# Eight recurrent scans moved into the attention's steps, and post-norms that multiply by their weights ahead of the scale

## The chip, the cores and the metric

The kernel runs on one core of one Trainium2 chip. A core has five engines with queues of their own: TensorE (PE in the profile; its weight loads are PEld), VectorE (DVE), ScalarE (ACT), GpSimd (POOL) and SyncE (SP, which here only issues transfers). Each engine works its queue in order and waits on semaphores for the others. The metric is the device time of one execution in microseconds; the kernel before takes 1060.09 us (median of 3 runs, 1060.06 to 1060.18).

## What is computed

Two encoder layers over a sequence of 512 tokens of 1024 channels in float32. Layer 0 mixes with attention and a recurrent branch side by side, layer 1 with a two-dimensional Fourier transform; each is followed by a SwiGLU. All four sublayers have a norm before and one after:

```python
x = x + rmsnorm(m, ln_mix_post[l])                 # m: the mixer of rmsnorm(x, ln_mix_pre[l])
x = x + rmsnorm(swiglu(hn, w_ffn_gate[l], w_ffn_up[l], w_ffn_down[l]), ln_ffn_post[l])

# attention of layer 0: 4 heads, two softmax maps each
p = jax.nn.softmax(s - slopes * dist, axis=-1)
a = p[:, :, 0] - lam * p[:, :, 1]
# recurrent branch: for a forward and a backward direction
a = jnp.exp(log_a)
u = jnp.sqrt(-jnp.expm1(2.0 * log_a)) * (i * x)
_, h = lax.associative_scan(_lin_combine, (a, u), axis=1, reverse=reverse)   # h[t] = a[t] h[t-1] + u[t]
rec = (h_fwd + h_bwd) * jax.nn.gelu(yg)
```

The recurrence has 512 channels, four tiles of 128, and two directions: eight scans over 512 positions. Attention and `rec` are joined and multiplied by the output matrix.

## The kernel before

Every matrix product is done in three matmuls (`mm3`, lines 108 to 111): each operand is split into a high part (`hi`, rounded) and a rest (`lo`), and hi*hi, hi*lo and lo*hi are added in PSUM. `split` (lines 100 to 106) makes the two parts: ACT casts (line 103, the `whi`, `qk`, `aT` of the profile), then DVE or POOL subtracts (line 106, `wlo`, `qk`, `aT`). Weights arrive as `raw` tiles by SP's queue and are split a few units ahead of their use; for units 8 to 13 (`LO_POOL`) the subtraction is POOL's, not DVE's.

Layer 0 goes in this order: pre-norm; projections for v, the recurrent input and its gates (`make_gates`); the decays (`lru_decay`, DVE, lines 487 to 489); the projection of q and k for heads 0 and 1 (`proj_qk(0)`); the square roots (ACT) and `ix*q` (POOL, line 497, `lru_root`). Then comes the attention loop, one step for each of 4 heads and 4 blocks of 128 queries, 16 steps (lines 680 to 690). A step i does:

- `scores`: six PE matmuls into two score banks (`psc`, line 550); DVE adds the bias and takes the row minimum (`p`, line 554, one for each map); ACT's exp (line 93); DVE's reciprocal and factor `c` (lines 558, 559), and one combination of the two maps (line 560)
- half of a filler product, 12 matmuls: heads 2 and 3's q and k in steps 0 to 7 (`pqk`), the GeLU gate's projection in steps 8 to 15 (`pyg`)
- in steps 0 to 3 two scans (`lru_scan`, line 502 forward, 505 backward); behind each backward one POOL adds the two directions (line 506, `hsum`)
- `finish_step`: the product with v for step i-3 if that is an odd block (`poT`, 12 matmuls), the transposition of step i-2's probabilities (`paT`, line 572, then an ACT cast and a DVE subtraction into `aT`), and now and then the head's norm and its transposition (`norm_o`, `turn_o`)

A scheduler lays this program out on the engines' queues by its own estimate of when things will be ready; it may place an instruction earlier or later than the code's order as long as the data allow. `order_after` (line 80) adds an edge that it must keep. PSUM has 8 banks, handed out in turn.

After the loop come the output projection, the first SwiGLU, the Fourier layer and the second SwiGLU, all bound to long chains of matmuls. Each ends in `proj_tok`, which finishes its four token tiles one after another and calls `post_norm` (line 255) for each: ACT squares both halves out of PSUM and sums, DVE scales the sum to the mean (lines 215, 216), POOL raises it to -0.5 (line 209), DVE multiplies each half out of PSUM by that and by the weights (line 265) and adds it to x (line 266). `pre_norm` or `pre_norm_tok` follows on the same tile, and in the last one the output transfers (line 860, all on SP).

Of the kernel before, what the change touches and what calls it, by code (L numbers as in the profile page):

```python
# [25 lines left out]
EPS = 1e-6  # L26
# [9 lines left out]
def encoder_kernel(  # L36
# [55 lines left out]
    def act(out_, in_, func, name, **kw):  # L92
        ins = A.activation(out_, in_, func, **kw)  # L93
# [27 lines left out]
    xt = [xpool.tile([P, D], F32, name=f"x{t}", tag=f"x{t}") for t in range(NT)]  # L121
# [79 lines left out]

    ident = const.tile([P, P], F32, name="ident")
    make_identity(nc, ident)
    mhalf = const.tile([P, 4], F32, name="mhalf")
    V.memset(mhalf, -0.5)

    def inv_sqrt(m):
        r = sm("r")
        G.tensor_tensor(out=r, in0=m, in1=mhalf[:, 0:1], op=ALU.pow)  # L209
        return r  # L210

    def inv_rms(ssa, ssb, n):

        m0, m = sm("m"), sm("m")
        V.tensor_scalar(out=m0, in0=ssa, scalar1=n * EPS, scalar2=None, op0=ALU.add)
        V.tensor_scalar(out=m, in0=ssb, scalar1=m0, scalar2=1.0 / n, op0=ALU.add, op1=ALU.mult)  # L216
        return inv_sqrt(m)

    def pre_stats(t, junk):
        ss = [sm("ss"), sm("ss")]  # L220
        for h in range(2):
# [33 lines left out]
    def post_norm(t, ps, g):  # L255

        ys = pair("y")
        ss = [sm("ss"), sm("ss")]
        for h in range(2):
            A.activation(ys[h], ps[h], AF.Square, accum_out=ss[h])  # L260
        r = inv_rms(ss[0], ss[1], D)
        for h in range(2):
            sl = slice(h * S, (h + 1) * S)
            y = ys[h]
            V.scalar_tensor_tensor(out=y, in0=ps[h], scalar=r, in1=g[:, sl], op0=ALU.mult, op1=ALU.mult)
            V.tensor_tensor(out=xt[t][:, sl], in0=xt[t][:, sl], in1=y, op=ALU.add)
# [103 lines left out]
    for name, ap in (  # L370
# [8 lines left out]
        n = ap.shape[0]  # L379
# [119 lines left out]
    def lru_scan(d, c):  # L499
        a_, q, u = lru_ac.pop((d, c))  # L500
        if d == 0:
            V.tensor_tensor_scan(out=u, data0=a_, data1=u, initial=0.0, op0=ALU.mult, op1=ALU.add)
            hsum[c] = u
        else:
            V.tensor_tensor_scan(out=u[:, ::-1], data0=a_[:, ::-1], data1=u[:, ::-1], initial=0.0, op0=ALU.mult, op1=ALU.add)  # L505
# [4 lines left out]
    bias = {}  # L510
# [25 lines left out]
    probs = {}  # L536
    sums = {}

    def scores(h, t):

        q_, k_ = qks[h]
        pr = pair("p")
        if t == 0:
            sums[h] = sm("sums", 8)
        s_ = sums[h]

        ps = [bank("psc"), bank("psc")]
        for n, (i, j) in enumerate(((0, 0), (0, 1), (1, 0))):
            for m, sl in enumerate(halves):
                T.matmul(ps[m], lhsT=q_[i][sl, t * P:(t + 1) * P], rhs=k_[j][sl, :], start=n == 0, stop=n == 2)  # L550
        for m in range(2):

            mn = sm("mn")
            V.tensor_tensor_reduce(out=pr[m], in0=ps[m], in1=bias[h][:, 384 - t * P:384 - t * P + S],  # L554
                                   op0=ALU.add, op1=ALU.min, scale=-1.0 / math.sqrt(QK), scalar=3.0e38, accum_out=mn)
            act(pr[m], pr[m], AF.Exp, "exp", scale=-1.0, bias=mn, accum_out=s_[:, m * NT + t:m * NT + t + 1])
        c1 = sm("c1")
        V.reciprocal(c1, s_[:, NT + t:NT + t + 1])
        V.scalar_tensor_tensor(out=c1, in0=c1, scalar=nlam, in1=s_[:, t:t + 1], op0=ALU.mult, op1=ALU.mult)
        V.scalar_tensor_tensor(out=pr[0], in0=pr[1], scalar=c1, in1=pr[0], op0=ALU.mult, op1=ALU.add)  # L560
        probs[h, t] = pr[0]
# [89 lines left out]
    lru = [(d, c) for c in range(4) for d in range(2)]  # L651
# [8 lines left out]
    n = len(steps)  # L660

    def finish_step(i):

        def step(lag):
            return steps[i - lag] if 0 <= i - lag < n else (None, None)

        h, t = step(3)
        if h is not None and t % 2:
            av(h, t // 2)
        h, t = step(2)  # L670
        if h is not None:
# [184 lines left out]
    proj_tok(range(8), lambda k: fT[k], 2, 6, fin1, turn_x)  # L856

    def after1(t):
        for h in range(2):
            nc.sync.dma_start(out[t * P:(t + 1) * P, h * S:(h + 1) * S], xt[t][:, h * S:(h + 1) * S])  # L860
# [63 lines left out]
```

## Time and profile before

| what | value |
|---|---|
| median of 3 runs | 1060.09 us (1060.06 to 1060.18) |
| the profiled execution's own time | 1061.07 us |
| its span, first to last instruction | 1059.2 us |
| mean granted TensorE clock | 0.992 |
| PE busy | 1027.0 us, 97% of the span |
| DVE busy | 478.0 us, 45% |
| ACT busy | 380.7 us, 36% |
| POOL busy | 100.1 us, 9% |

The span is what the trace shows; the execution's own time has 1.87 us more around it. A row of the timeline gives start, duration, engine, line, operation and tiles, and in brackets the idle time ahead of it with the instruction that ended it. Rows that merge several instructions end in xN. Matmuls overlap their neighbours, so the distance from one start to the next tells their pace. A row of the view by stretches gives, after its length, the busy time of each engine (number of instructions), then the granted clock (1.00 is full), the DMA share and GB/s. A row of the groups gives busy time and mean nanoseconds of one instruction, and the idle time ahead of them.

### The profile page before, as it was taken

What the parts mean: (1) busy time and instruction counts of PE and PEld (TensorE: products, weight loads), DVE (VectorE), ACT (ScalarE), POOL (GpSimd) and SP (SyncE); (2) the same over time, 40 slices, a digit from 0 to 9 for tenths busy, and PEclk for the clock granted to TensorE, in tenths of its full rate; (3) what the DMA queues carried; (4) which work ended last, traced back from release to release, by engine and by line L of the source; (5) the groups of instructions that cost most, each with busy time, mean ns of one, the idle gap of its engine ahead of it and who ended that gap; (6) DMA issues with size and microseconds to landing.
All of it is one profiled execution on the core that took longest, in us unless ns stands there. A gap on an engine that the chain in (4) does not pass through costs nothing.

```text
span 1059.2 us, 12273 instructions
## 1 busy us (share of the span) xinstructions
PE 1027.0 (97%) x4945; PEld 856.9 (81%) x4945; DVE 478.0 (45%) x720; ACT 380.7 (36%) x628; POOL 100.1 (9%) x94
## 2 busy tenths in 40 slices
PE   5999699999999999999999999999999999999997
PEld 5897577779888888888888888898888888888885
DVE  5969767754542322223333456645322223234304
ACT  5385456733532221123233445334321123223201
POOL 1058423211000000000100110100000000000000
PEclk9999899999999999999999999999999999999999
DMA  6531212321652343222533015027243223224002
GB/s 221 164 118 56 87 48 83 112 66 41 188 170 80 93 127 99 80 80 80 164 115 119 1 60 160 1 80 218 84 136 100 80 80 105 94 80 133 6 1 80
DMA packets 73123, 102.93 MB, mean 97 GB/s; under 512 B 3893, under 2 KB 61290, under 8 KB 73066
## 3 DMA queue, kind: packets, MB, share of 16 engines
q1 hardware_dynamic: 70442, 94.02, 28.4%
q0 software_dynamic: 2624, 8.13, 2.2%
q8 instruction: 39, 0.64, 0.2%
q14 instruction: 18, 0.15, 0.0%
HBM read 100.04 MB, written 2.10 MB: 96 GB/s over the span
## 4 chain that ended last, share of the span: by engine, by line
PE 86%; DVE 6%; ACT 4%; issue 1%; POOL 1%; DMA 1%; SPq 0%; POOLq 0%; DVEq 0%; ACTq 0%
PE pc L110 15%; PE pc L109 15%; PE pc L111 15%; PE pj L111 10%; PE pj L110 10%; PE pj L109 10%; ACT p L93 1%; ACT whi L103 1%; DVE gate L505 1%; DMA raw<-in_w_in_dram 1%; DVE p L560 1%; PE pT L250 1%; DVE wlo L106 1%; PE put L109 1%; PE put L110 1%
## 5 line engine op out<-in xcount | busy, mean ns | idle before, releaser
L106 DVE TENSOR_TENSOR wlo<-raw,whi 128x1024 fp32r<-128x1024 f32 x158 | 192.0, 1239 | 272.8 <-ACT whi L103 221.6
L110 PE MATMUL pc<-hnlo,whi 128*128 128x512 f32 (+1 forms) x768 | 285.2, 372 | 0.0
L109 PE MATMUL pc<-hnhi,whi 128*128 128x512 f32 (+1 forms) x768 | 284.6, 372 | 0.5 <-ACT hnhi L103 0.5
L111 PE MATMUL pc<-hnhi,wlo 128*128 128x512 f32 (+1 forms) x768 | 285.0, 371 | 0.0
L103 ACT CAST whi<-raw 128x1024 fp32r<-128x1024 f32 x164 | 167.9, 1050 | 121.4 <-PE pj L110 31.1
L110 PEld LDWEIGHTS pc<-hnlo,whi 128*128 128x128 f32 x768 | 144.7, 188 | 25.5 <-DVE hnlo L106 0.4
L109 PEld LDWEIGHTS pc<-hnhi,whi 128*128 128x128 f32 x768 | 144.2, 188 | 26.0 <-ACT hnhi L103 1.0
L111 PEld LDWEIGHTS pc<-hnhi,wlo 128*128 128x128 f32 x768 | 144.7, 188 | 24.6
L111 PE MATMUL pj<-whi,gs 128*128 128x512 f32 x352 | 137.0, 389 | 0.0
L109 PE MATMUL pj<-whi,gs 128*128 128x512 f32 x352 | 137.0, 389 | 0.0
L110 PE MATMUL pj<-wlo,gs 128*128 128x512 f32 x352 | 137.0, 389 | 0.0
L93 ACT ACTIVATE gated<-pc 128x512 f32<-128x512 f32 x44 | 26.2, 597 | 271.9 <-PE pc L111 271.9
L721 DVE TENSOR_TENSOR gated<-gated,pc 128x512 f32<-128x512 f32 x44 | 30.2, 686 | 113.3 <-PE pc L111 113.3
L109 PEld LDWEIGHTS pj<-whi,gs 128*128 128x128 f32 x352 | 66.1, 188 | 13.8
L111 PEld LDWEIGHTS pj<-whi,gs 128*128 128x128 f32 x352 | 66.1, 188 | 13.7
L110 PEld LDWEIGHTS pj<-wlo,gs 128*128 128x128 f32 x352 | 66.1, 188 | 13.6
L209 POOL TENSOR_TENSOR r<-m,mhalf 128x1 f32<-128x1 f32 x32 | 17.5, 545 | 552.3 <-DVE m L216 552.3
L260 ACT ACTIVATE y<-pj 128x512 f32<-128x512 f32 x32 | 19.1, 596 | 82.3 <-PE pj L111 82.3
L103 ACT CAST gs<-gated 128x512 fp32r<-128x512 f32 x44 | 25.3, 618 | 52.1 <-PE pj L110 32.2
L106 DVE TENSOR_TENSOR gs<-gated,gs 128x512 fp32r<-128x512 f32 x44 | 28.4, 685 | 31.3 <-ACT gs L103 31.3
L93 ACT ACTIVATE p<-p,mn 128x512 f32<-128x512 f32 x32 | 22.9, 719 | 37.5 <-DVE mn L554 37.5
L106 POOL TENSOR_TENSOR wlo<-raw,whi 128x1024 fp32r<-128x1024 f32 x12 | 28.8, 2407 | 51.5 <-ACT whi L103 51.5
(184 smaller groups left out, 1255.5 us busy)
## 6 DMA issues: line engine op xcount, KB each, us to landing
raw<-in_w_ffn_gate_dram SPq DMA_DIRECT2D x44, 512.0 KB, 3.9
raw<-in_w_ffn_up_dram SPq DMA_DIRECT2D x44, 512.0 KB, 4.9
raw<-in_w_ffn_down_dram SPq DMA_DIRECT2D x44, 512.0 KB, 3.4
raw<-in_w_in_dram SPq DMA_DIRECT2D x20, 512.0 KB, 3.8
raw<-in_w_mix_out_dram SPq DMA_DIRECT2D x8, 512.0 KB, 3.3
raw<-in_w_fourier_out_dram SPq DMA_DIRECT2D x8, 512.0 KB, 4.2
pos<-in_dft_pos_dram POOLq DMA_DIRECT2D x8, 256.0 KB, 5.1
out_dram<-x SPq DMA_DIRECT2D x8, 256.0 KB, 2.1
```

The source lines that it names most:

```text
L93: ins = A.activation(out_, in_, func, **kw)
L103: A.copy(hi, src)
L106: lo_eng.tensor_tensor(out=lo, in0=src, in1=f(hi), op=ALU.subtract)
L109: T.matmul(ps, lhsT=l[0], rhs=r[0], start=start, stop=False)
L110: T.matmul(ps, lhsT=l[0], rhs=r[1], start=False, stop=False)
L111: T.matmul(ps, lhsT=l[1], rhs=r[0], start=False, stop=stop)
L209: G.tensor_tensor(out=r, in0=m, in1=mhalf[:, 0:1], op=ALU.pow)
L250: T.transpose(pt[:, k * P:(k + 1) * P], xh[:, k * P:(k + 1) * P], ident)
L260: A.activation(ys[h], ps[h], AF.Square, accum_out=ss[h])
L505: V.tensor_tensor_scan(out=u[:, ::-1], data0=a_[:, ::-1], data1=u[:, ::-1], initial=0.0, op0=ALU.mult, op1=ALU.add)
L560: V.scalar_tensor_tensor(out=pr[0], in0=pr[1], scalar=c1, in1=pr[0], op0=ALU.mult, op1=ALU.add)
L721: V.tensor_tensor(out=gated[fc], in0=gated[fc], in1=ps, op=ALU.mult)
```

## The change

It has four edits.

1. The eight scans no longer stand two by two in steps 0 to 3 but one in each of steps 1, 2, 4, 5, 7, 8, 10 and 11, and each gets an order edge behind the last score tile (line 554) of its step, so that the scheduler can't pull it ahead.
2. The norms scale inside the square (ACT's `scale`, 1/sqrt(1024)), so that the mean is two plain additions.
3. `post_norm` multiplies PSUM by the weights first (a new DVE pass into `y`), squares into a scrap tile `junk`, and afterwards scales and adds in one pass on SBUF alone.
4. The second half of each output tile goes out by ACT's queue in place of SP's.

```diff
-    def inv_rms(ssa, ssb, n):
+    RD = 1.0 / math.sqrt(D)
+    def inv_rms(ssa, ssb):
-        m0, m = sm("m"), sm("m")
-        V.tensor_scalar(out=m0, in0=ssa, scalar1=n * EPS, scalar2=None, op0=ALU.add)
-        V.tensor_scalar(out=m, in0=ssb, scalar1=m0, scalar2=1.0 / n, op0=ALU.add, op1=ALU.mult)
-        return inv_sqrt(m)
+        m0, m, r = sm("m"), sm("m"), sm("r")
+        V.tensor_scalar(out=m0, in0=ssa, scalar1=EPS, scalar2=None, op0=ALU.add)
+        V.tensor_tensor(out=m, in0=ssb, in1=m0, op=ALU.add)
+        G.tensor_tensor(out=r, in0=m, in1=mhalf[:, 0:1], op=ALU.pow)
+        return r
...
     def post_norm(t, ps, g):
         for h in range(2):
-            A.activation(ys[h], ps[h], AF.Square, accum_out=ss[h])
-        r = inv_rms(ss[0], ss[1], D)
+            V.tensor_tensor(out=ys[h], in0=ps[h], in1=g[:, h * S:(h + 1) * S], op=ALU.mult)
+            A.activation(junk, ps[h], AF.Square, scale=RD, accum_out=ss[h])
+        r = inv_rms(ss[0], ss[1])
         for h in range(2):
-            V.scalar_tensor_tensor(out=y, in0=ps[h], scalar=r, in1=g[:, sl], op0=ALU.mult, op1=ALU.mult)
-            V.tensor_tensor(out=xt[t][:, sl], in0=xt[t][:, sl], in1=y, op=ALU.add)
+            V.scalar_tensor_tensor(out=xt[t][:, sl], in0=ys[h], scalar=r, in1=xt[t][:, sl], op0=ALU.mult, op1=ALU.add)
...
     def lru_scan(d, c):
+        order_after(sc, [last_score[0]])
...
-            V.tensor_tensor_reduce(out=pr[m], in0=ps[m], in1=bias[h][:, 384 - t * P:384 - t * P + S],
+            last_score[0] = V.tensor_tensor_reduce(out=pr[m], in0=ps[m], in1=bias[h][:, 384 - t * P:384 - t * P + S],
...
+    scans = list(lru)
     for i in range(n):
         scores(*steps[i])
-        if 2 * i < len(lru):
-            lru_scan(*lru[2 * i])
-            lru_scan(*lru[2 * i + 1])
+        if i % 3 and scans:
+            lru_scan(*scans.pop(0))
...
     def after1(t):
-        for h in range(2):
-            nc.sync.dma_start(out[t * P:(t + 1) * P, h * S:(h + 1) * S], xt[t][:, h * S:(h + 1) * S])
+        for h, q in enumerate((nc.sync, A)):
+            q.dma_start(out[t * P:(t + 1) * P, h * S:(h + 1) * S], xt[t][:, h * S:(h + 1) * S])
```

PE's queue is the same before and after. The first place is DVE's queue ahead of the first attention step. The scans are the rows that read and write one `gate` tile; `qk_140` is the rest of head 1's k, `p_141` is step 0's first score tile. Before:

```order
L106 TENSOR_TENSOR wlo_133_902<-raw_131_899,whi_132_901 128x1024
L502 SCALAR_TENSOR_TENSOR gate_85_551<-gate_85_551 128x512
L106 TENSOR_TENSOR wlo_136_908<-raw_134_905,whi_135_907 128x1024
L505 SCALAR_TENSOR_TENSOR gate_88_563<-gate_88_563 128x512
L106 TENSOR_TENSOR qk_138_936<-pqk_137_911,qk_138_936 128x512
L502 SCALAR_TENSOR_TENSOR gate_93_607<-gate_93_607 128x512
L505 SCALAR_TENSOR_TENSOR gate_96_619<-gate_96_619 128x512
L502 SCALAR_TENSOR_TENSOR gate_107_695<-gate_107_695 128x512
L505 SCALAR_TENSOR_TENSOR gate_110_707<-gate_110_707 128x512
L502 SCALAR_TENSOR_TENSOR gate_113_719<-gate_113_719 128x512
L505 SCALAR_TENSOR_TENSOR gate_116_731<-gate_116_731 128x512
L106 TENSOR_TENSOR qk_140_964<-pqk_139_939,qk_140_964 128x512
```

Now, from the same `wlo` on:

```order
L106 TENSOR_TENSOR wlo_133_903<-raw_131_900,whi_132_902 128x1024
L106 TENSOR_TENSOR wlo_136_909<-raw_134_906,whi_135_908 128x1024
L106 TENSOR_TENSOR qk_138_937<-pqk_137_912,qk_138_937 128x512
L106 TENSOR_TENSOR qk_140_965<-pqk_139_940,qk_140_965 128x512
L558 ISA p_141_984,mn_145_994<-psc_143_986,bias_125_840 128x512
```

And further on, from step 1's second score tile (`p_156`; `p_163` is step 2's first) on:

```order
L558 ISA p_156_1031,mn_160_1043<-psc_158_1033,bias_125_840 128x512
L558 ISA mn_160_1043 128x1
L501 SCALAR_TENSOR_TENSOR gate_85_552<-gate_85_552 128x512
L562 RECIPROCAL c1_161_1046<-sums_142_985 128x1
L558 ISA p_163_1066,mn_166_1075<-psc_164_1067,bias_125_840 128x512
```

All eight scans stood ahead of `qk_140`; now none does, and each stands between its step's score tiles and the reciprocal that waits for ACT's exp.

The second place is POOL's queue over the attention: `gate` rows are the additions of the two directions, `wlo` rows the split weights, `r4` the norm of a head. Before:

```order
L506 TENSOR_TENSOR gate_85_551<-gate_85_551,gate_88_563 128x512
L506 TENSOR_TENSOR gate_93_607<-gate_93_607,gate_96_619 128x512
L506 TENSOR_TENSOR gate_107_695<-gate_107_695,gate_110_707 128x512
L506 TENSOR_TENSOR gate_113_719<-gate_113_719,gate_116_731 128x512
L106 TENSOR_TENSOR wlo_150_1006<-raw_148_1003,whi_149_1005 128x1024
L106 TENSOR_TENSOR wlo_153_1012<-raw_151_1009,whi_152_1011 128x1024
```

Now:

```order
L106 TENSOR_TENSOR wlo_150_1007<-raw_148_1004,whi_149_1006 128x1024
L106 TENSOR_TENSOR wlo_153_1013<-raw_151_1010,whi_152_1012 128x1024
L524 DMA bias_154_1016<-in_alibi_dram 128x896
L524 DMA bias_169_1085<-in_alibi_dram 128x896
L508 TENSOR_TENSOR gate_85_552<-gate_85_552,gate_88_564 128x512
L106 TENSOR_TENSOR wlo_191_1175<-raw_189_1172,whi_190_1174 128x1024
L106 TENSOR_TENSOR wlo_194_1181<-raw_192_1178,whi_193_1180 128x1024
L508 TENSOR_TENSOR gate_93_608<-gate_93_608,gate_96_620 128x512
L106 TENSOR_TENSOR wlo_240_1401<-raw_238_1398,whi_239_1400 128x1024
```

The additions stood in a row ahead of the weights; now each waits for its second scan between two weights.

The third place is ACT's queue at the last two token tiles and the program's end, with what each row waits for (a number behind an engine's name is its semaphore). Before:

```order
L260 ACTIVATE y_1211_7710,ss_1212_7711<-pj_1125_7006 128x512 [waits DVE_49,PE_49]
L260 ACTIVATE y_1211_7710,ss_1213_7712<-pj_1126_7007 128x512 [waits PE_49,Pool_49]
L260 ACTIVATE y_1217_7751,ss_1218_7752<-pj_1127_7008 128x512 [waits DVE_49,PE_49]
L260 ACTIVATE y_1217_7751,ss_1219_7753<-pj_1128_7009 128x512 [waits PE_49,Pool_49]
L920 UNCONDITIONAL_BRANCH
```

Now:

```order
L261 ACTIVATE junk_92,ss_1212_7712<-pj_1125_7007 128x512 [waits DVE_49,Activation_49]
L261 ACTIVATE junk_92,ss_1213_7713<-pj_1126_7008 128x512 [waits DVE_49,Activation_49,Pool_49]
L864 DMA out_0_dram<-x2_81 128x512 [waits DVE_49]
L261 ACTIVATE junk_92,ss_1218_7753<-pj_1127_7009 128x512 [waits DVE_49,Activation_49]
L261 ACTIVATE junk_92,ss_1219_7754<-pj_1128_7010 128x512 [waits DVE_49,Activation_49,Pool_49]
L864 DMA out_0_dram<-x3_82 128x512 [waits DVE_49]
```

The square of a bank waited for PE; now it waits for DVE, whose multiplication of that same bank stands ahead of it, and not for PE. Tile 2's output transfer now stands in ACT's queue ahead of tile 3's squares.

More of the change, by code (lines that the diff above doesn't have):

```diff
@@ L203, in encoder_kernel @@
     make_identity(nc, ident)
+    junk = const.tile([P, S], F32, name="junk")
     mhalf = const.tile([P, 4], F32, name="mhalf")
     V.memset(mhalf, -0.5)
-    def inv_sqrt(m):
-        r = sm("r")
+    RD = 1.0 / math.sqrt(D)
[3 more added lines that the diff above has]
+        V.tensor_tensor(out=m, in0=ssb, in1=m0, op=ALU.add)
         G.tensor_tensor(out=r, in0=m, in1=mhalf[:, 0:1], op=ALU.pow)
         return r
-    def inv_rms(ssa, ssb, n):
-        m0, m = sm("m"), sm("m")
-        V.tensor_scalar(out=m0, in0=ssa, scalar1=n * EPS, scalar2=None, op0=ALU.add)
-        V.tensor_scalar(out=m, in0=ssb, scalar1=m0, scalar2=1.0 / n, op0=ALU.add, op1=ALU.mult)
-        return inv_sqrt(m)
     def pre_stats(t, junk):
@@ L221, in pre_stats @@
         for h in range(2):
-            A.activation(junk[h], xt[t][:, h * S:(h + 1) * S], AF.Square, accum_out=ss[h])
-        return inv_rms(ss[0], ss[1], D)
+            A.activation(junk[h], xt[t][:, h * S:(h + 1) * S], AF.Square, scale=RD, accum_out=ss[h])
+        return inv_rms(ss[0], ss[1])
     hn = {}
@@ L259, in post_norm @@
         for h in range(2):
-            A.activation(ys[h], ps[h], AF.Square, accum_out=ss[h])
-        r = inv_rms(ss[0], ss[1], D)
+            V.tensor_tensor(out=ys[h], in0=ps[h], in1=g[:, h * S:(h + 1) * S], op=ALU.mult)
+            A.activation(junk, ps[h], AF.Square, scale=RD, accum_out=ss[h])
+        r = inv_rms(ss[0], ss[1])
         for h in range(2):
             sl = slice(h * S, (h + 1) * S)
-            y = ys[h]
-            V.scalar_tensor_tensor(out=y, in0=ps[h], scalar=r, in1=g[:, sl], op0=ALU.mult, op1=ALU.mult)
-            V.tensor_tensor(out=xt[t][:, sl], in0=xt[t][:, sl], in1=y, op=ALU.add)
+            V.scalar_tensor_tensor(out=xt[t][:, sl], in0=ys[h], scalar=r, in1=xt[t][:, sl], op0=ALU.mult, op1=ALU.add)
     def proj_tok(ks, lhs, chunk, tail, finish, late=None, hook=None, spare=False):
@@ L501, in lru_scan @@
         if d == 0:
-            V.tensor_tensor_scan(out=u, data0=a_, data1=u, initial=0.0, op0=ALU.mult, op1=ALU.add)
+            sc = V.tensor_tensor_scan(out=u, data0=a_, data1=u, initial=0.0, op0=ALU.mult, op1=ALU.add)
             hsum[c] = u
         else:
-            V.tensor_tensor_scan(out=u[:, ::-1], data0=a_[:, ::-1], data1=u[:, ::-1], initial=0.0, op0=ALU.mult, op1=ALU.add)
+            sc = V.tensor_tensor_scan(out=u[:, ::-1], data0=a_[:, ::-1], data1=u[:, ::-1], initial=0.0, op0=ALU.mult, op1=ALU.add)
+        order_after(sc, [last_score[0]])
+        if d:
             G.tensor_tensor(out=hsum[c], in0=hsum[c], in1=u, op=ALU.add)
@@ L537, in encoder_kernel @@
     sums = {}
+    last_score = [None]
     def scores(h, t):
```

## The prediction

> **What bounds the kernel now.** I read the page first, then the stretches, then PE's waits, then the timeline of the worst stretch. The page's first rows put PE at 97%, so what can be gained is PE's idle time and its slow clock:
>
> ```profile
> PE 1027.0 (97%) x4945; PEld 856.9 (81%) x4945; DVE 478.0 (45%) x720; ACT 380.7 (36%) x628; POOL 100.1 (9%) x94
> ```
>
> The stretches show where that is. These three are the start of the attention, its middle and a place near its end:
>
> ```profile
> 105.60:135.00 29.40, 20.78 (x85) 15.18 (x84) 22.75 (x47) 13.95 (x31) 14.30 (x9) 0.83 0.27 87
> 135.00:180.00 45.00, 45.00 (x259) 35.13 (x257) 30.79 (x75) 28.94 (x64) 12.46 (x7) 1.00 0.13 46
> 180.00:190.00 10.00, 7.95 (x36) 6.30 (x37) 8.38 (x14) 5.55 (x12) 3.93 (x3) 0.83 0.48 157
> ```
>
> In the first PE lacks 8.6 of 29.4 us and runs at 0.83 of its clock; in the middle it never stops and DVE is free 14.2 us of 45. PE's timeline names the waits, and the score products (`psc`) count the steps (step 1 at 100.83, 2 at 104.67, 8 at 147.58, 9 at 153.34, 10 at 158.06):
>
> ```profile
> 100.83 0.97 PE L550 MATMUL psc<-qk,qk 64*128 64x512 f32 x6
> 104.67 0.96 PE L550 MATMUL psc<-qk,qk 64*128 64x512 f32 x6
> 109.77 0.50 PE L109 MATMUL pqk<-hnhi,whi 128*128 128x512 f32 x1 [4.13 <-DVE qk L106]
> 115.84 0.66 PE L572 MATMUL paT<-ident,p 128*128 128x128 f32 x4 [1.47 <-DVE p L560]
> 126.66 0.38 PE L109 MATMUL poT<-aT,v 128*128 128x256 f32 x1 [1.92 <-ACT aT L103]
> 128.14 0.58 PE L110 MATMUL poT<-aT,v 128*128 128x256 f32 x1 [1.10 <-DVE aT L106]
> 147.58 0.97 PE L550 MATMUL psc<-qk,qk 64*128 64x512 f32 x6
> 153.34 0.96 PE L550 MATMUL psc<-qk,qk 64*128 64x512 f32 x6
> 158.06 0.97 PE L550 MATMUL psc<-qk,qk 64*128 64x512 f32 x6
> ```
>
> The first wait is for `qk`, which DVE had queued behind all eight scans. Here are the scans' two groups, with least, median and most ns, and DVE's and ACT's rows behind them:
>
> ```profile
> L502 DVE TENSOR_TENSOR_SCAN gate<-gate x4: 1673/2234/2314, 89.4 to 104.8; 128x512 f32<-128x512 f32 x4
> L505 DVE TENSOR_TENSOR_SCAN gate<-gate x4: 2215/2246/2310, 93.8 to 106.9; 128x512 f32<-128x512 f32 x4
> 109.05 0.66 DVE L106 TENSOR_TENSOR qk<-pqk,qk 128x512 fp32r<-128x512 f32 x1
> 110.35 0.73 ACT L93 ACTIVATE p<-p,mn 128x512 f32<-128x512 f32 x1 [10.42 <-DVE mn L554]
> 109.64 0.68 DVE L554 CUSTOM_DVE_ANT_0 p<-psc,bias 128x512 f32<-128x512 f32 x1
> 112.88 2.91 DVE L560 SCALAR_TENSOR_TENSOR p<-p,c 128x512 f32<-128x512 f32 x1
> ```
>
> Step 0's scores were ready near 98 (a step of 3.84 ahead of step 1's 100.83, then 0.96 for the products), and DVE took them up at 109.64; ACT, whose exp comes next, had stood still since 99.93. The waits at 115.84 to 128.14 are the same lateness working off.
>
> **The change part by part.**
>
> *What the scans cost now.* At full clock a step lasts 3.84 us with nothing behind it (100.83 to 104.67), 4.72 with `paT` and four more transpositions (153.34 to 158.06), 5.76 with `poT` and `paT` (147.58 to 153.34). `paT` alone is half of 4.72 - 3.84, so a step with it lasts 4.28. From step 1 to step 8 that makes 3.84 + 4.28 + 4.28 + 5.76 + 4.28 + 5.76 + 4.72 = 32.9 us; it took 147.58 - 100.83 = 46.75. So the lateness costs **13.9 us**, waits and slow clock together, and this is the most that edit 1 can give.
>
> *What a scan costs in its new place.* All eight ran with POOL busy. Alone, none is in the trace. Three POOL rows, and DVE's `wlo` group, bound it:
>
> ```profile
> 56.99 2.54 POOL L471 TENSOR_TENSOR gate<-gate,xc 128x512 f32<-128x512 f32 x2 [31.87 <-ACT gate L93]
> 84.47 17.11 POOL L497 TENSOR_TENSOR gate<-gate,th 128x512 f32<-128x512 f32 x8 [9.13 <-ACT th L93]
> 110.44 4.80 POOL L106 TENSOR_TENSOR wlo<-raw,whi 128x1024 fp32r<-128x1024 f32 x2
> L106 DVE TENSOR_TENSOR wlo<-raw,whi 128x1024 fp32r<-128x1024 f32 x158 | 192.0, 1239 | 272.8 <-ACT whi L103 221.6
> ```
>
> A POOL multiplication takes 1.27 alone and 2.14 beside the scans: eight lose 7.0 us, in which DVE ran five scans and two `wlo`. With 1.24 for each `wlo`, a scan holds POOL off 0.9. The lower bound is 0.69, an ordinary pass over a tile of that size (the `aT` row below), the upper 2.25. I take 1.1, next to the 0.9 of the rows in which the two take turns, and count what POOL makes it wait apart.
>
> *What covers it.* DVE's groups of the middle stretch, with idle time ahead:
>
> ```profile
> L554 DVE CUSTOM_DVE_ANT_0 p<-psc,bias 128x512 f32<-128x512 f32 x16 | 10.5, 682 | 0.0
> L560 DVE SCALAR_TENSOR_TENSOR p<-p,c 128x512 f32<-128x512 f32 x8 | 6.0, 752 | 0.3
> L106 DVE TENSOR_TENSOR aT<-paT,aT 128x512 fp32r<-128x512 f32 x8 | 5.5, 686 | 4.9 <-ACT aT L103 4.9
> L558 DVE RECIPROCAL c<-sums 128x1 f32<-128x1 f32 x8 | 1.3, 164 | 7.6 <-ACT p L93 7.6
> ```
>
> Each reciprocal waits 0.95 us for ACT's exp. The scan now stands in that hole, so alone it costs DVE 0.15 us a step. But POOL stands in the way: `p` (line 560) takes 0.75, and took 2.91 at 112.88, while POOL ran two `wlo` from 110.44 to 115.24. Four `hsum` (1.27) now stand between POOL's `wlo` (2.40) too, each held for its second scan; `wlo_191` waits behind the first, but is used only in step 8.
>
> *Step by step with these durations.* PE reaches 104.67 as before. `qk` is done at 98.2 (its product ends at 97.0, then a cast and a subtraction), so the 4.13 goes. Step 0's exps start where ACT is free, at 99.9, and end at 101.4; factor and `p` end at 102.5, where 115.8 stood. ACT then casts a weight, and POOL's `wlo` of it runs to 104.9; step 1's scan waits for that. Step 2's scan waits for nothing, but behind it the first `hsum` holds step 2's `p` to 112.0. Step 3 has no scan; the `aT` pair of steps 0 and 1 is ready at 117.1, and PE's `poT` asks at 116.8: 0.3 to 0.4 lost. Step 4's scan waits for `wlo_191` to 119.3, its `p` for `wlo_194` to 123.3, step 5's `p` for the second `hsum`; the second `aT` pair comes at 129.6, and PE asks at 126.8: **2.8 lost**. From step 6 on DVE keeps up by this reckoning: two of three steps have a scan, POOL's next `wlo` come only in steps 8 and 9, and DVE's 14.2 free us in 45 take 6 x 1.1. What a 2 us wait does is seen near the attention's end:
>
> ```profile
> 161.85 0.28 PE L109 MATMUL poT<-aT,v 128*128 128x256 f32 x1
> 163.81 0.96 PE L550 MATMUL psc<-qk,qk 64*128 64x512 f32 x6
> 185.12 0.38 PE L110 MATMUL poT<-aT,v 128*128 128x256 f32 x1 [2.05 <-DVE aT L106]
> 189.48 0.50 PE L109 MATMUL pyg<-hnhi,whi 128*128 128x512 f32 x1
> 181.63 2.83 DVE L560 SCALAR_TENSOR_TENSOR p<-p,c 128x512 f32<-128x512 f32 x1
> ```
>
> From `poT` through `psc` took 4.36 us there (185.12 to 189.48), 2.92 at full clock (163.81 + 0.96 - 161.85): some **1.5** more, which I add for the slow clock behind the 2.8. The Trainium skill's "TensorE: Matmul & The Clock Gate" (Part 1: The HAM clock gate) has the clock fall after an idle window of about 3.4 us; by it a wait of 2.8 would cost nothing further, and the time would come out 1.5 us lower. This trace disagrees: 2.05 us was enough, with 0.83 granted over 180 to 190. That wait itself comes from a `p` held by POOL (2.83 at 181.63), which no edit touches, and I leave it in. Edit 1 in sum: 13.9 - 0.4 - 2.8 - 1.5 = **9.2 us**.
>
> *Post-norm at the end.* The timeline after the last matmul (done near 1051.5), and groups for the new operations:
>
> ```profile
> 1051.61 0.60 ACT L260 ACTIVATE y<-pj 128x512 f32<-128x512 f32 x1 [2.09 <-PE pj L111]
> 1053.26 1.41 DVE L265 SCALAR_TENSOR_TENSOR y<-pj,r,gpost 128x512 f32<-128x512 f32 x2 [0.72 <-POOL r L209]
> 1054.59 1.28 DVE L266 TENSOR_TENSOR x<-x,y 128x512 f32<-128x512 f32 x2
> 1055.29 0.94 SPq L860 DMA_DIRECT2D out_dram<-x  x2
> L721 DVE TENSOR_TENSOR gated<-gated,pc 128x512 f32<-128x512 f32 x44 | 30.2, 686 | 113.3 <-PE pc L111 113.3
> L242 DVE SCALAR_TENSOR_TENSOR xn<-x,r,gpre 128x512 f32<-128x512 f32 x8 | 5.7, 748 | 2.9 <-POOL r L209 2.9
> ```
>
> The square waits for the multiplication of its own bank, so the two are not beside each other: 0.69 more ahead of the square. Behind POOL the two additions go, 1.28 less 0.08 of overlap, and the scaling stays at two passes of 0.75. Net about -0.5, and the last transfer no longer stands behind the other on SP: **-0.55**, between -0.9 (issue alongside) and +0.3 (ACT's issue dearer than SP's 0.47). Under the squares' `scale` and the plain addition nothing changes on the path.
>
> *Post-norms in the middle.* The last pre-norm after the first of them, and PE's turning of it:
>
> ```profile
> 253.40 1.42 DVE L242 SCALAR_TENSOR_TENSOR xn<-x,r,gpre 128x512 f32<-128x512 f32 x2 [0.74 <-POOL r L209]
> 259.60 0.45 PE pT L250 x4
> ```
>
> It is ready near 254.8 and taken up at 259.60: 4.8 us of cover, so these cost nothing. With that cover gone the added 0.69 less the additions' 1.2 would still be no loss, and the bank comes free at the square, ahead of POOL.
>
> All together -9.75 us. The profiled execution's 1061.07 would be 1051.3; it stands 0.98 above the median, so the median 1060.09 becomes **1050.3**.
>
> **The rivals.**
>
> *No new wait.* DVE keeps pace everywhere; POOL's `wlo` fall elsewhere. For it: the trace shows PE without a stop from 135 to 180. 13.9 + 0.55 gives 1045.6.
>
> *DVE becomes the bound.* If a scan takes 2.25 here too, a scan step costs DVE 3.7 (the groups above, with `qk` every second) + 2.25 = 5.95 against PE's mean (5.76 + 4.28) / 2 = 5.0: six such steps from 4 on lose 0.95 each, 5.7; steps 1 and 2, where PE's step is 4.06 on average, 3.8; the four steps between, at 3.7 + 0.95 for the exp, win back 0.35 each: 8 in all, and the slow clock once, 1.5. That leaves 13.9 + 0.55 - 9.5 = 5: 1055.1.
>
> *Slower.* Place: the `poT` of every second step from 4 to 14, which wants both `aT` parts of two blocks. If POOL holds DVE in each pair of steps, PE waits 2.05 and then runs slowly 1.5, as at 185.12: 3.55 each. Four lose 14.2 of the 14.45 gained; from the fifth the kernel is slower; with six 1060.1 - 14.45 + 21.3 = 1066.9. "SBUF — State Buffer" of the Trainium skill (Who interferes with whom) speaks for it: DVE with two SBUF inputs and POOL exclude each other for a whole instruction, whoever starts first; the 2.91 at 112.88 agrees. Against it: POOL was busy 12.5 of 45 us in the middle and PE lost nothing, and the four `hsum` add 5.1.
>
> *It does nothing.* Step 0 might wait for something else, ACT's table load before its first exp or the biases, and the lateness stay: 1059.5. Against it: ACT had stood still for 10.42 us when DVE's first minimum released it at 110.35.
>
> **How the numbers follow.** A measurement of this kernel tells about 0.2% (2.1 us) from no change. Forecast 0.57, no new wait 0.13, DVE-bound 0.20, slower 0.06, nothing 0.04. The range from 1045.5 to 1056 holds the first three save their edges, 0.82 or so. Faster 0.90, same 0.04, slower 0.06.
>
> **What would show it.** Right: step 0's `p` near 98.3, no wait of PE between 104.7 and 116, `psc` of step 8 near 138 in place of 147.58, scans of about 1.1 us where POOL is idle, a wait of 2 to 3 us ahead of `poT` in step 6, and the last square starting 0.7 after the last matmul. Wrong: PE waits for `aT` in most `poT` steps, scans of 2.2 with POOL idle, or a step 8 later than 143.

## The result, and the profile after

The changed kernel takes **1051.75 us** in the median of 4 runs (1051.39 to 1052.72), the kernel before 1060.07 (1058.67 to 1060.18, 4 runs); the medians lie 8.3 us apart. The ratio, which is taken over all runs and not from the medians, is 0.9926 (95% interval 0.9909 to 0.9943), or 7.8 us. The profiled execution took 1051.39 us with a span of 1049.6; before it was 1061.07 and 1059.2, so the two traces differ by 9.7 and 9.6 us.

The page's first row (busy us, share of the span) and the three stretches (length, then busy time of PE, PEld, DVE, ACT and POOL, then PE's granted clock, DMA share, GB/s):

```profile
PE 1023.3 (97%) x4945; PEld 853.7 (81%) x4945; DVE 472.9 (45%) x720; ACT 381.5 (36%) x628; POOL 95.2 (9%) x94
```

```profile
105.60:135.00 29.40, 27.21 (x140) 20.36 (x139) 26.95 (x53) 14.55 (x33) 7.41 (x4) 0.94 0.26 85
135.00:180.00 45.00, 41.96 (x239) 32.53 (x238) 35.75 (x74) 28.03 (x63) 19.91 (x10) 1.00 0.23 71
180.00:190.00 10.00, 9.29 (x53) 7.29 (x51) 7.28 (x16) 7.74 (x14) 6.25 (x3) 1.00 0.36 109
```

In the first stretch PE works 27.21 us where it worked 20.78, with a clock of 0.94 in place of 0.83. But the middle, where PE had never stopped, now lacks 3.04 us. The marks for the balance are the first score product of a step (`psc`; step 0 at 96.32, steps 4, 5 and 6 at 112.55, 118.54 and 122.87, step 7 at 131.48, step 8 at 137.27, steps 14 and 15 at 168.70 and 178.21), PE's two long waits inside the loop, the first position product of the second layer (`put`) and the last matmul. First the changed kernel's rows of PE, then five of the kernel before that the prediction does not show (its steps 0, 14 and 15, `put` and the last matmul):

```profile
96.32 0.97 PE L554 MATMUL psc<-qk,qk 64*128 64x512 f32 x6
112.55 0.96 PE L554 MATMUL psc<-qk,qk 64*128 64x512 f32 x6
118.54 0.97 PE L554 MATMUL psc<-qk,qk 64*128 64x512 f32 x6
122.87 0.96 PE L554 MATMUL psc<-qk,qk 64*128 64x512 f32 x6
129.08 0.38 PE L110 MATMUL poT<-aT,v 128*128 128x256 f32 x1 [2.19 <-DVE aT L106]
131.48 1.65 PE L554 MATMUL psc<-qk,qk 64*128 64x512 f32 x6
137.27 0.97 PE L554 MATMUL psc<-qk,qk 64*128 64x512 f32 x6
168.70 1.44 PE L554 MATMUL psc<-qk,qk 64*128 64x512 f32 x6
176.26 0.39 PE L110 MATMUL poT<-aT,v 128*128 128x256 f32 x1 [3.04 <-DVE aT L106]
178.21 0.96 PE L554 MATMUL psc<-qk,qk 64*128 64x512 f32 x6
600.78 0.39 PE L109 MATMUL put<-pos,hnhi 128*128 128x512 f32 x1
1042.02 0.39 PE L111 MATMUL pj<-whi,gs 128*128 128x512 f32 x1
```

```profile
96.99 0.97 PE L550 MATMUL psc<-qk,qk 64*128 64x512 f32 x6
179.00 0.97 PE L550 MATMUL psc<-qk,qk 64*128 64x512 f32 x6
188.26 1.29 PE L550 MATMUL psc<-qk,qk 64*128 64x512 f32 x6
609.88 0.39 PE L109 MATMUL put<-pos,hnhi 128*128 128x512 f32 x1
1051.12 0.39 PE L111 MATMUL pj<-whi,gs 128*128 128x512 f32 x1
```

The 9.6 us of the spans come together from six stretches. Up to step 0: 0.67 gained. Step 0 to step 8: 50.59 before, 40.95 now, 9.64 gained. Step 8 to 15: 40.68 and 40.94, 0.26 lost. Step 15 to `put`: 421.62 and 422.57, 0.95 lost. `put` to the last matmul: 441.24 both times, nothing. Last matmul's start to the span's end: 8.08 and 7.58, 0.50 gained. So the attention's start gave nearly all, and about 1.2 us of it was given back near the attention's end: from step 8 to step 14 both kernels take 31.4 us, and all of the 1.2 lies behind step 14.

On VectorE the scans (lines 501 and 504), the factor `c` and the combination `p` show what is in the way. Of POOL the rows that were running beside them follow:

```profile
103.17 2.21 DVE L501 TENSOR_TENSOR_SCAN gate<-gate 128x512 f32<-128x512 f32 x1
107.96 1.22 DVE L504 TENSOR_TENSOR_SCAN gate<-gate 128x512 f32<-128x512 f32 x1
109.27 1.30 DVE L563 SCALAR_TENSOR_TENSOR c<-c,nlam,sums 128x1 f32<-128x1 f32 x1
117.68 1.89 DVE L501 TENSOR_TENSOR_SCAN gate<-gate 128x512 f32<-128x512 f32 x1
119.91 2.79 DVE L564 SCALAR_TENSOR_TENSOR p<-p,c 128x512 f32<-128x512 f32 x1
125.75 1.29 DVE L563 SCALAR_TENSOR_TENSOR c<-c,nlam,sums 128x1 f32<-128x1 f32 x1
128.34 0.68 DVE L106 TENSOR_TENSOR aT<-paT,aT 128x512 fp32r<-128x512 f32 x1
172.80 2.81 DVE L564 SCALAR_TENSOR_TENSOR p<-p,c 128x512 f32<-128x512 f32 x1
```

```profile
101.87 2.44 POOL L106 TENSOR_TENSOR wlo<-raw,whi 128x1024 fp32r<-128x1024 f32 x1 [1.44 <-issue]
109.26 1.28 POOL L508 TENSOR_TENSOR gate<-gate,gate 128x512 f32<-128x512 f32 x1 [3.89 <-PE psc L554]
119.72 2.44 POOL L106 TENSOR_TENSOR wlo<-raw,whi 128x1024 fp32r<-128x1024 f32 x1 [1.23 <-ACT whi L103]
125.74 1.29 POOL L508 TENSOR_TENSOR gate<-gate,gate 128x512 f32<-128x512 f32 x1 [3.58 <-DVE c L562]
167.99 7.06 POOL L106 TENSOR_TENSOR wlo<-raw,whi 128x1024 fp32r<-128x1024 f32 x3 [2.19 <-ACT whi L103]
```

A scan with POOL idle takes 1.22; beside POOL's subtraction 2.21 and 1.89. A factor of one column takes 0.22, and 1.30 when POOL's sum started 0.01 us ahead of it. `p` takes 0.75, and 2.79 from 119.91, when POOL had begun a subtraction at 119.72. Behind that `p` the second pair of `aT` came late, and PE waited 2.19 at 129.08. The other wait, 3.04 at 176.26, stands behind the `p` at 172.80, held by the last of three subtractions in a row. The kernel before has three in a row there too:

```profile
176.82 7.10 POOL L106 TENSOR_TENSOR wlo<-raw,whi 128x1024 fp32r<-128x1024 f32 x3 [2.24 <-ACT whi L103]
```

There they began 2.18 us ahead of step 14's `psc` and PE's wait was 2.05; now they begin only 0.71 ahead of it.

The end, ACT's square and VectorE's operations after the last matmul (done near 1042.41):

```profile
1042.45 0.69 DVE L260 TENSOR_TENSOR y<-pj,gpost 128x512 f32<-128x512 f32 x1 [1.01 <-PE pj L111]
1043.25 0.60 ACT L261 ACTIVATE junk<-pj 128x512 f32<-128x512 f32 x1 [1.04 <-DVE m L214]
1044.86 1.41 DVE L265 SCALAR_TENSOR_TENSOR x<-y,r,x 128x512 f32<-128x512 f32 x2 [0.72 <-POOL r L216]
```

The square begins 0.84 after the last matmul, behind the multiplication of its bank, and nothing follows the two passes into `x` but their transfers.

### The profile page after: what moved, and what is told of

Its sections match the earlier page's. It is cut to its first block, busy times and chain, and to the rows that moved or that the text cites. A ratio compares the mean times of both kernels' runs of the same rounds, so it can differ in the third digit from the quotient of the medians.

```text
span 1049.6 us, 12279 instructions
## 1 busy us (share of the span) xinstructions
PE 1023.3 (97%) x4945; PEld 853.7 (81%) x4945; DVE 472.9 (45%) x720; ACT 381.5 (36%) x628; POOL 95.2 (9%) x94
## 4 chain that ended last, share of the span: by engine, by line
PE 88%; DVE 6%; ACT 3%; issue 1%; POOL 1%; DMA 1%; SPq 0%; DVEq 0%; POOLq 0%; ACTq 0%
PE pc L110 15%; PE pc L109 15%; PE pc L111 15%; PE pj L111 10%; PE pj L110 10%; PE pj L109 10%; DVE p L558 1%; DVE p L564 1%; ACT whi L103 1%; ACT p L93 1%; PE pqk L109 1%; PE pqk L110 1%; PE pqk L111 1%; PE pT L250 1%; DMA raw<-in_w_in_dram 1%
## 5 line engine op out<-in xcount | busy, mean ns | idle before, releaser
L261 ACT ACTIVATE junk<-pj 128x512 f32<-128x512 f32 x32 | 19.2, 598 | 94.9 <-DVE y L260 57.8
L260 DVE TENSOR_TENSOR y<-pj,gpost 128x512 f32<-128x512 f32 x32 | 22.0, 689 | 56.5 <-PE pj L111 56.4
```

The source lines that it names most:

```text
L260: V.tensor_tensor(out=ys[h], in0=ps[h], in1=g[:, h * S:(h + 1) * S], op=ALU.mult)
L261: A.activation(junk, ps[h], AF.Square, scale=RD, accum_out=ss[h])
```

## The experiments

Each of the eleven runs computes the whole of the reference. Ratios are to the kernel before, run beside it on the same chip, with 95% intervals; its medians are 1059.66 us for the first four runs, 1058.75 for the next four and 1060.20 for the last three, so times from different groups are compared by their ratios or by their traces. Steps are counted from the first `psc` of step 0, so that differences ahead of the attention drop out: step 8 comes 50.59 us after step 0 in the kernel before and 40.95 in the changed one.

**The scans' edits alone.** The kernel before, with edit 1 and none of the others.

> The kernel before with the scans' edits alone (one scan in a step, i % 3, each held behind its step's last score tile); post-norms, scale and output queues as before. Theory (the gain is the attention's start, and the post-norms give 0.55 at the end): about 1052.3 us, 0.5 above the changed kernel, with psc of step 8 still near 137.3 and 7.7 us from the last matmul to the span's end. Rival (the post-norms give nothing, or lose): 1051.2 to 1051.8. Rival (they also give in the middle of the program, or at its start): 1053 or more.

Measured: 1051.98 us, ratio 0.9927 (0.9913 to 0.9940). Step 8 comes 39.43 us after step 0 (96.10 to 135.53), earlier than in the changed kernel because the lower clock did not follow the wait of step 6 here; and from the last matmul's end (1041.68) to the span's end (1049.4) there are 7.7 us, as before. So edit 1 carries the gain. The times alone can't tell 0.5 from nothing; the trace does it in the tail.

**The other edits alone.** The changed kernel, with the scans as before (the order edge is out as well):

```diff
...
-        if i % 3 and scans:
-            lru_scan(*scans.pop(0))
+        if 2 * i < len(lru):
+            lru_scan(*lru[2 * i])
+            lru_scan(*lru[2 * i + 1])
```

> The changed kernel with the scans put back as before (two in each of steps 0 to 3, no edge); post-norms, scale and output queues as changed. Theory: 1059.5 us, 0.5 under the kernel before, from the tail alone (7.2 us from last matmul to the end in place of 7.7). Rival (post-norms give nothing): 1060.1. Rival (a gain in the middle or at the start too): 1058.5 or less.

Measured: 1059.01 us, ratio 0.9994 (0.9985 to 1.0003). From the last matmul's end (1050.42) to the span's end (1057.6) there are 7.2 us. The tail gives 0.5 by both traces, and the time agrees with it without proving it. One row of this run is needed further down, PE's wait in step 14, which here was not followed by the lower clock:

```profile
184.29 0.39 PE L110 MATMUL poT<-aT,v 128*128 128x256 f32 x1 [2.07 <-DVE aT L106]
```

**No edge.** The changed kernel with `order_after(sc, [last_score[0]])` taken out.

> The changed kernel without the ordering edge: the code still writes one scan in a step, but nothing holds a scan behind the score tiles, and VectorE's row has all eight scans ahead of the last qk split of the first heads again. Theory (it is the place on VectorE that counts): the 4 us wait ahead of the first psc comes back, and the time is 1059 to 1060, with only the post-norms' 0.5 left. Rival (one scan in a step in the code is enough): 1052.

Measured: 1059.51 us, ratio 0.9992 (0.9983 to 1.0002). PE's wait is back, in step 2 (the expectation puts it ahead of the first `psc`):

```profile
109.40 0.57 PE L109 MATMUL pqk<-hnhi,whi 128*128 128x512 f32 x1 [4.17 <-DVE qk L106]
```

The code still writes one scan in a step, but the scheduler puts all eight ahead of the last `qk`. The edge is what makes the change; without it, moving the line in the code did nothing.

**Two scans in a step, behind the score tiles.**

```diff
-        if i % 3 and scans:
-            lru_scan(*scans.pop(0))
+        if 2 * i < len(lru):
+            lru_scan(*lru[2 * i])
+            lru_scan(*lru[2 * i + 1])
```

Here the edge of the changed kernel stays.

> The changed kernel with two scans in each of the first four steps instead of one in two of three, each still held behind its step's last score tile. Theory (VectorE's load in a step counts: two scans of 1.2 to 2.2 us on top of 3.9 us of own work are more than the 4 us that TensorE takes for a step): the first psc still starts near 96.5, but steps 1 to 4 come late one by one, psc of step 8 at 141 to 145, time 1055 to 1058. Rival (only the 4.1 us wait ahead of the first psc and the slow clock behind it count): psc of step 8 near 137 to 138, 1052.

Measured: 1056.6 us, ratio 0.9972 (0.9960 to 0.9984); step 8 at 142.78, 47.40 after step 0. First DVE's rows in steps 0 and 1, then PE's:

```profile
97.93 2.66 DVE L501 TENSOR_TENSOR_SCAN gate<-gate 128x512 f32<-128x512 f32 x1
100.51 1.19 DVE L504 TENSOR_TENSOR_SCAN gate<-gate 128x512 f32<-128x512 f32 x1
103.13 2.85 DVE L564 SCALAR_TENSOR_TENSOR p<-p,c 128x512 f32<-128x512 f32 x1
```

```profile
120.77 0.58 PE L109 MATMUL poT<-aT,v 128*128 128x256 f32 x1 [4.12 <-ACT aT L103]
123.73 0.58 PE L110 MATMUL poT<-aT,v 128*128 128x256 f32 x1 [2.38 <-DVE aT L106]
```

Step 0 is on time (`psc` at 95.38), and its `p` is done at 106 in place of 102. The lateness that the edge took away comes back at the first `poT`. So VectorE's load in each step decides, and spreading the scans was worth nearly 5 us of the 8.

**No subtraction on POOL.**

```diff
-LO_POOL = (8,9,10,11,12,13)
+LO_POOL = ()
```

> The changed kernel with the weights' subtractions that GpSimd did (units 8 to 13) on VectorE. Theory (GpSimd at work holds VectorE's operations with two operands from SBUF): inside the loop the two long waits of p (2.79 and 2.81 us) shrink to about 0.75, scans all take about 1.2; but each subtraction costs VectorE 1.2 us, and in 105 to 135 us the stall removed (some 2.7 us) is about the work added (2.4 us), so the wait at poT of step 6 stays near 2 us and the time stays within 1 us of 1051.75. Rival (the stalls were the bottleneck, and the added work finds idle VectorE): 1048 to 1049. Rival (the stalls of p have another cause): p still takes 2.8 us in places, and with the added work the time is 1054 or more.

Measured: 1049.61 us, ratio 0.9912 (0.9899 to 0.9926). PE's wait in step 6, and the two stretches that the expectation speaks of:

```profile
129.03 0.39 PE L110 MATMUL poT<-aT,v 128*128 128x256 f32 x1 [1.64 <-DVE aT L106]
```

```profile
105.00:135.00 30.00, 28.22 (x153) 21.31 (x150) 27.72 (x57) 15.95 (x37) 2.57 (x2) 1.00 0.16 51
135.00:180.00 45.00, 43.98 (x248) 34.00 (x247) 37.81 (x84) 28.89 (x64) 6.49 (x4) 1.00 0.23 71
```

All `p` of the loop take 0.75 but one (1.67, beside a sum), so POOL had held them. In step 6 the reckoning was right: stall out, work in, 1.64 for 2.19. But the expected "within 1 us" was missed: the time is 2.1 us under 1051.75, 1.5 by the ratios. The intervals of the two ratios overlap, so the traces have to tell it: from the first `psc` to `put` there are 502.22 us here and 504.46 in the changed kernel, 2.2 less. The reckoning looked only at step 6, and the gain lies behind it: in the middle stretch PE lacks 1.0 in place of 3.0, and step 15 comes 7.48 us behind step 14 in place of 9.51, since VectorE had room for the work in steps 8 to 15 and the three subtractions in a row are gone.

**All scans late.**

```diff
-        if i % 3 and scans:
+        if i >= 6 and scans:
```

> The changed kernel with all eight scans in steps 6 to 13, none in steps 1 to 5. Theory (the wait of 2.2 us at poT of step 6 is what the scans of steps 1 to 5 left VectorE behind by): psc of step 8 near 133 to 135 in place of 137.3, and since VectorE works 35.75 of 45 us from 135 to 180, most of the four more scans there (4.9 us) find room: 1048 to 1050. Rival (the later steps have no room, or buffers held longer stop the loads): the same wait comes back behind step 8, 1051 to 1055. Rival (the wait of step 6 is GpSimd's doing alone): psc of step 8 stays near 137.

Measured: 1051.87 us, ratio 0.9938 (0.9924 to 0.9951). PE does not stop before step 8, which starts at 133.59, 36.72 after step 0: 4.2 better than in the changed kernel. Then:

```profile
149.70 0.39 PE L110 MATMUL poT<-aT,v 128*128 128x256 f32 x1 [1.12 <-DVE aT L106]
176.15 0.58 PE L110 MATMUL poT<-aT,v 128*128 128x256 f32 x1 [3.97 <-DVE aT L106]
```

```profile
166.91 8.04 POOL L106 TENSOR_TENSOR wlo<-raw,whi 128x1024 fp32r<-128x1024 f32 x3 [2.19 <-PE pmT L614]
```

So the wait of step 6 was the scans' doing, as the theory had it, and the time was the second theory's: the four us are given back, to waits of 1.12 and 3.97 and the lower clock behind the second (step 15 comes 82.78 us after step 0, 81.89 in the changed kernel; `put` comes 504.05 after it, 504.46 there). Who comes to step 14 early meets the same three subtractions there: they begin 0.07 us behind its `psc` here.

**Squares first.** In `post_norm` both squares and `inv_rms` come ahead of the two multiplications by the weights:

```diff
         for h in range(2):
-            V.tensor_tensor(out=ys[h], in0=ps[h], in1=g[:, h * S:(h + 1) * S], op=ALU.mult)
             A.activation(junk, ps[h], AF.Square, scale=RD, accum_out=ss[h])
         r = inv_rms(ss[0], ss[1])
+        for h in range(2):
+            V.tensor_tensor(out=ys[h], in0=ps[h], in1=g[:, h * S:(h + 1) * S], op=ALU.mult)
```

> The changed kernel with the post-norms' two squares ahead of their two multiplications by the weights. Theory (the last square waits 0.7 us for the multiplication of the same PSUM bank): the last square starts within 0.15 us of the last matmul's end in place of 0.8, from the last matmul to the span's end 6.5 to 6.6 us in place of 7.2, time 1051.1. Rival (the square waits for something else, or the multiplication then delays the last x): 7.2 us, 1051.75 or more.

Measured: 1050.76 us, ratio 0.9925 (0.9912 to 0.9937). The time can't show so little, but the trace can. The last square of ACT:

```profile
1042.77 0.60 ACT L260 ACTIVATE junk<-pj 128x512 f32<-128x512 f32 x1 [2.05 <-PE pj L111]
```

The last matmul is done at 1042.65 here and the span ends at 1049.1: 0.12 to the square and 6.45 us in all, 0.74 less than in the changed kernel. The multiplication now runs beside POOL's power.

**Two scans early, six late.** After the loop over `lru_root`, two scans without an edge; the other six in steps 6 to 11:

```diff
...
+    for dc in lru[:2]:
+        lru_scan(*dc)
...
-    scans = list(lru)
+    scans = lru[2:]
...
-        if i % 3 and scans:
+        if i >= 6 and scans:
```

> The changed kernel with two scans ahead of the last heads' qk splits, where VectorE stands idle for 4.7 us, and the other six in steps 6 to 11; none in steps 1 to 5. Theory: the first psc still starts near 96.3, no wait at poT of step 6, psc of step 8 near 133 to 135, and behind it two scans fewer than with all eight late: 1047.5 to 1049.5. Rival (the two early scans stand in the way of the first qk splits while GpSimd multiplies, 2.2 us each): first psc later by 1 to 4 us, 1051 to 1053. Rival (the steps from 6 have no room): 1051 to 1053 with a wait behind step 8.

Measured: 1050.49 us, ratio 0.9921 (0.9908 to 0.9935), 1 us over what the theory allows, and with that chip's quicker kernel before the ratio is that of the changed kernel. `psc` of step 0 stays in place (96.64), though POOL makes each early scan 2.3 us long. But they are not free: POOL's multiplications end later, its first sum and two subtractions now run from 99.40 to 105.38, and step 0's `p` is held till 105.9 in place of 102.0; PE then waits 1.10 at 118.24. Step 8 comes 38.29 us after step 0, 2.7 better than in the changed kernel and 1.6 worse than with all scans late. The waits of 1.11 at 151.15 and 3.07 at 175.79, the latter with the lower clock behind it, take it back. As with the late scans, POOL's subtractions set the end.

**The three together**: no subtraction on POOL, two scans early and six late, squares first.

> The changed kernel with three things together: no weights' subtraction on GpSimd, two scans early and six in steps 6 to 11, squares ahead of the multiplications. Theory (VectorE falls behind in steps 1 to 5 by the scans there, in the later steps by GpSimd's subtractions, and the tail's square waits 0.65): no wait at poT of step 6, psc of step 8 near 133, waits of under 2 us behind it, 6.45 us after the last matmul: 1046.5 to 1048.5, ratio to the kernel before 0.988 to 0.990. Rival (the four scans put into steps 6 to 11 and the subtractions together are too much for VectorE there): a wait of 2 us or more behind step 8, 1049 to 1051.

Measured: **1047.61 us**, ratio 0.9883 (0.9867 to 0.9898); the changed kernel on the same chip has 0.9926 (0.9912 to 0.9940). PE's waits inside the loop, us in all, times, longest:

```profile
PE poT L110 <- DVE aT L106: 1.9, 2, 1.1
PE psc L555 <- DVE aT L106: 1.4, 2, 0.9
PE poT L109 <- ACT aT L103: 1.4, 1, 1.4
```

Step 8 comes 36.72 us after step 0 and step 15 77.88 (81.89 in the changed kernel), and the tail is 6.4. It beats both kernels, by 12.6 us and by 4.3. Where that comes from, the traces tell best. From the first `psc` to `put` the changed kernel takes 504.46 us, with two scans early and six late 503.95, without POOL's subtractions 502.22, with both 501.54; the tail gives 0.8 more. So the subtractions are worth 2.2 of it and the scans' new places 0.5 to 0.7: the parts add up, and nothing here shows that one makes the other worth more. No two of the three were run together without the third.

**The last unit on POOL again**: the same with `LO_POOL = (13,)`.

> The same, with the last unit's subtraction (13) on GpSimd again. Theory (on VectorE it brought waits of 1.3 and 0.8 us at 182 to 184 us): those two waits shrink to 0.4 in all, and the time is 0.5 to 1.5 us under the kernel with none on GpSimd. Rival (GpSimd holds VectorE there by as much): the same time.

Measured: 1048.26 us, ratio 0.9891 (0.9877 to 0.9905): not faster, and the rival holds. Of the two waits only the second shrank, from 0.81 to 0.34; the first stayed at 1.35, and waits of 0.87 for `oT` and 0.45 for `aT` appeared at 188.87 and 191.67, where there were none.

**The changed kernel again.**

> The changed kernel as it is, once more, for a ratio from the same chip as the two combinations, and for a second trace of the same waits. Theory: ratio to the kernel before 0.9915 to 0.9935; TensorE's waits are again 2.2 us in step 6 and 3.0 us in step 14, but the lower clock may follow another of them than in the first trace (0.39 against 0.58 us for the same 128x256 matmul), since with the same waits of other kernels it followed now the one and now the other. Rival (the clock is set by the wait alone): the lower clock again behind the wait of step 6 and not behind that of step 14.

Measured: 1051.89 us, ratio 0.9926 (0.9912 to 0.9940). The waits are 2.18 and 3.05, and the lower clock again follows the first and not the second: `psc` of step 7 takes 1.65 and step 8 comes 5.74 behind it. In these two traces of one kernel it did not move, as the rival has it. Two traces can't tell that it never does: the runs of the kernel without the edge go from 1056.92 us, with a mean granted clock of 0.996, to 1060.38 with 0.992, as if it came in some and not in others. And the kernel with the squares first has the same waits (2.17 and 3.03) at the same distance from step 0, and there the first leaves the clock alone. First the `psc` of steps 7 and 8 in the second trace of the changed kernel, then the same two with the squares first:

```profile
130.85 1.65 PE L554 MATMUL psc<-qk,qk 64*128 64x512 f32 x6
136.59 0.97 PE L554 MATMUL psc<-qk,qk 64*128 64x512 f32 x6
```

```profile
131.81 0.96 PE L555 MATMUL psc<-qk,qk 64*128 64x512 f32 x6
136.53 0.97 PE L555 MATMUL psc<-qk,qk 64*128 64x512 f32 x6
```

The step between them is 5.74 us in the one and 4.72, its full clock, in the other.

## Why the prediction was right

**What bounds it, and the ceiling of 13.9.** The lateness came from the scans ahead of `qk`: without the edge it is back (4.17), with it gone. That the whole 13.9 was the scans' is shown by the late scans and by the three together: from step 0 to step 8 both take 36.72 us, 13.87 less than the kernel before.

**A scan alone, 1.1.** It takes 1.22 where POOL is idle and up to 2.21 beside it in this kernel. 1.1 was short by a tenth, the upper bound 2.25 is what POOL makes of it, and 0.69 was far off.

**Step by step.** The 4.13 goes, and no wait of PE stands between 104.7 and 116. The first loss, 0.3 to 0.4 at step 4, measured 0.23 (112.55 to 118.54, less 5.76). Scans, sums and subtractions met as the prediction had them: `c` held at 109.27, the scan of step 4 to 119.6, its `p` to 122.7 (123.3 forecast), `c` again at 125.75. The second `aT` pair came at 129.0 and PE lost 2.19 in place of 2.8. With the lower clock, step 6 to step 8 took 14.40 against 10.48 at full clock: 3.9 lost, 4.3 forecast. All together step 0 to step 8 gave 9.64, **9.2 forecast**.

**The lower clock behind the wait, 1.5.** It measured 1.7 in this kernel (3.9 less 2.19). The Trainium skill's window of about 3.4 us ("TensorE: Matmul & The Clock Gate", Part 1: The HAM clock gate) would have put nothing behind a wait of 2.2, and here the trace went against that reading. But the term was not certain: with the scans alone, or the squares first, the same wait left the clock alone, so that it came here as forecast was luck in part. Nor does the price stay: step 8 comes 1.5 us earlier in those two kernels (39.43 and 39.39 after step 0), but step 14 only 0.8 (71.62 and 71.58, 72.38 here), because PE then loses more in step 10 (6.5 us for it, 5.8 here).

**"From step 6 on DVE keeps up"** was the step that failed, and only in part. Up to step 14 it holds. But the wait there, which the prediction left in at 2.05 as one "which no edit touches", grew to 3.04. Like is compared with like in the kernel with the other edits alone, whose wait is 2.07 and where the lower clock stayed away as it does here: step 15 comes 8.07 us behind step 14 there and 9.51 here, 1.4 lost, and behind step 15 the two are equal (422.55 and 422.57 to `put`). The three subtractions are not touched by the edit, but their place is: they come 1.5 us later, measured from step 14, since POOL's power for the head's norm begins 3.92 us ahead of step 14 (164.78) and began 5.44 ahead (173.56); ACT's `oT` waits for it, and the casts that the subtractions need stand behind that. The scans alone don't do that: without POOL's subtractions, with the scans in the same places, it is 5.40 again.

In the kernel before, the lower clock followed that wait and cost 1.2 (9.26 in place of 8.07), but 0.9 of it came back: VectorE and ACT had that time to catch up, and the waits of 0.34 for the last `poT` and 0.92 for the last head's `oT` that the changed kernel has were none and 0.59. This shows in every trace with a wait of 2 us or more there: step 15 to `put` takes 421.3 to 421.6 in the seven in which the lower clock followed it, 422.5 to 422.6 in the three in which it did not. So 0.95 of the 1.2 us given back appears behind step 15, but was lost in step 14. The 1.2 us are most of what lies between the 9.75 forecast and the 8.3 of the medians. The profiled pair seems to hit the forecast (9.7) only because the start was 0.67 us shorter in that execution.

That 0.67 is no work of the change. PE's first wait for `xn` is 9.2 us in the kernel before, 8.5 and 7.9 in the two traces of the changed kernel, 7.7 with the scans alone and 9.0 with the other edits alone; it ends when the first weights of the norms have landed.

**Post-norm at the end, -0.55** measured -0.50, with the square 0.84 behind the last matmul (0.7 forecast). Nothing in the middle: from `put` to the last matmul there is no difference at all.

**The rivals.** A kernel without any new wait (1045.6) did not come; the three together come nearest to it, with 1047.61. VectorE as the bound (1055.1) did not come either; two scans in a step come near it, with 1056.6. POOL holding every `poT` step did not come: two of six, though by the mechanism described. The Trainium skill's exclusion ("SBUF — State Buffer", Who interferes with whom) held at every subtraction and sum of POOL in the changed kernel's loop, down to an operation of one column. One row goes against it: a `c` of 0.22 us at 143.43 ran inside POOL's power of four columns (142.29 to 144.18).

## What to carry to other kernels

A scheduler sorts by what is ready, so an operation that is ready early and needed late is put in front of the one that the bounding engine waits for; an order edge holds it back, and here moving the scans gained nothing without it. Spread such work by the room in each step, and look at what POOL does there: its work cost VectorE as well, at places that the share of busy time (9%) does not show. And count a gain where it arrives, not where it starts, since an engine that comes early meets the next fixed thing early.

## What the runs showed that was not expected

- The lower clock of TensorE (a 128x256 matmul each 0.21 us in place of 0.12) does not follow from the length of a wait between 2 and 3 us. The same wait of 2.2 us at the same place of the program was followed by it in two traces of the changed kernel and not with the scans alone or the squares first; of the waits of 3.0 it followed those of the latter two and neither of the former; of 2.05 and 2.07 near the end it followed the first, in the kernel before, and not the second, with the other edits alone. What decides, the runs leave open.
- What the lower clock costs depends on what waits behind it. In step 14 it cost 1.4 us up to step 15 (10.86 with the squares first, 9.51 in the changed kernel), but only 0.2 up to `put` (432.30 and 432.08 from step 14): later waits shrank by about as much.
- A VectorE operation on 128x1 numbers, 0.22 us long, takes 1.30 when POOL's sum began 0.01 us earlier: POOL's time is the price, not the operation's own size.
- Taking POOL's twelve subtractions of 2.4 us each over to VectorE, which does one in 1.2, took 2.2 us off the traces from the first `psc` to `put`, although VectorE was the engine that PE waited for.
